# A hybrid attention block on one core: x's first slice in two transfers, small loads moved, first kv products reordered, gate stores on ScalarE's queue, last sum of squares in one step

## The chip, the cores and the metric

The kernel runs on one core of one Trainium2 chip. A core has five engines that run side by side, each with its own instruction queue: TensorE (PE in the profile; PEld is its weight load), VectorE (DVE), ScalarE (ACT), GpSimd (POOL) and SyncE (SP), which here only issues transfers. Transfers may be issued from SP, ACT and POOL; all of them run on the core's 16 DMA engines. The metric is the device time of one execution in microseconds; lower is better.

## The reference

One pre-norm residual layer, 512 tokens, width 1024, all float32. One input projection feeds two token mixers: A, latent attention with 8 heads, dense and causal by chunks of 64; and B, sparse attention, in which an indexer scores the keys, each query keeps its best 128, and a relative-position bias is added. Each branch is gated, projected and weighted by a sigmoid gate; the sum goes through an output projection, the residual is added, and a final RMS norm closes it.

```python
h = rmsnorm(x, norm_g[l])
(q_lat, c_kv, k_rope, z_a, q_b, k_b, v_b, z_b,
 q_idx, k_idx, w_idx, gate_a, gate_b) = jnp.split(h @ w_in[l], cuts, axis=-1)
q = (rmsnorm(q_lat, g_q_lat[l]) @ w_uq[l]).reshape(B, S, MLA_HEADS, MLA_NOPE + MLA_ROPE)
kv = (rmsnorm(c_kv, g_kv_lat[l]) @ w_ukv[l]).reshape(B, S, MLA_HEADS, MLA_NOPE + MLA_V)
...
y_a = mla_attention(q_nope, q_pe, k_nope, k_pe, v_a, pos).reshape(B, S, MLA_WIDTH) * jax.nn.silu(z_a)
y_b = dsa_attention(q_b, k_b, v_b, q_idx, k_idx, w_idx, rel_bias, pos, topk) * jax.nn.silu(z_b)
merged = (jax.nn.sigmoid(gate_a) * (y_a @ w_o_a[l])
          + jax.nn.sigmoid(gate_b) * (y_b @ w_o_b[l]))
x = x + merged @ w_out[l]
return rmsnorm(x, final_g)
```

## The kernel before

Every float32 operand of a product is split into a high part, rounded to TensorE's fast float format (a cast on ACT, L302, or a scaled copy, L311), and a low part, the rest (a subtraction on DVE or POOL, L328 and L330, or DVE's `scalar_tensor_tensor`, L339). A product is then three matmuls (`mm3`): high by high, high by low, low by high. Lines such as L302, L311, L328, L339 and L400 are helpers that record every operation of their kind, so tiles tell more than lines. Large square products (gates, some projections, the output projection) are done in Strassen's way with seven block products instead of eight (`seven`, `output`).

The order of instructions on each engine is fixed when the program is built. Each piece of the work is a generator (a thread) that yields steps with an estimated duration; `Flow.run` simulates the engines with these estimates and always emits the step that can start first, with a small bias for a thread's priority and a tiny random nudge per thread, drawn from a generator seeded with `DRAW`. So any change of a step's estimate, of a thread's steps or of the seed may change the order anywhere. Tiles come from pools of buffers (`slot`, `RAW`, `bank`); a buffer is given back by `put`.

The stages, in order:

- Start. `setup` issues the first index-query weights (`w_qi`, 128 KB) on ACT's queue; `loads` issues on SP, for each of 8 slices k of the model width, x transposed (`xT[k]`, 128 rows of 512 tokens, 256 KB), index weights and kv weights, with `norm_g` behind the first x; `setup_pool` issues the identity matrix (64 KB) and the latent gains (`g_lat`, 2.5 KB) on POOL's queue. `warm_up` runs 15 matmuls on zeros. `early_x` makes scaled high and low parts of each x slice, `early_w` those of the weights.
- `early_mm` multiplies them: index products `qi` (128 by 384 outputs, two groups of three matmuls each slice) and kv products (four token tiles, 328 columns, three matmuls each: 12 a slice), then the q latents. For slice 0 the high part of x is made in three pieces (`PIECES`: tokens 256 to 511, 128 to 255, 0 to 127), so that four high-by-high index matmuls can begin early; the low part is made in one instruction for all 512 tokens, and kv products wait for both parts of x and both parts of the weights.
- In the meantime x is loaded once more by rows, its sums of squares are taken (`x_squares`), and `rstd` is turned and spread over all partitions.
- Middle: normalised x, the remaining projections, the indexer's scores, top-k by repeated maximum on DVE (`topk`), and both kinds of attention heads. The eight tiles of the first sigmoid gate (`w_ga`) are computed early, stored to a scratch area in DRAM (`spilt`) and fetched back when they are needed (`fetch_gates`).
- End: gated branch outputs, output projection, and per token tile t: `finish` adds a block product to the residual (L339), takes a sum of squares into a column of `ssf[t]`, and multiplies by the final gain; `scale_out` adds the partial sums of squares, takes the power -1/2 on POOL (L378), scales both halves (DVE and ACT) and stores them from SP. Tiles 2 and 3 are finished first, then 0 and 1. For tiles 1 and 3 the output's second half arrives in two pieces, so there are three partial sums (`count == 3`), and the third takes an add of its own; the third of tile 1 is the last product of the kernel, and its squares are summed on DVE (`last`), the others on ACT:

```python
        yield ts(rs[:, 0:1], ssf[t][:, 0:1], ssf[t][:, 1:2], D * EPS, ALU.add, ALU.add)
        if count == 3:
            yield is_done(("sq", t, 2))
            yield tt(rs[:, 0:1], rs[:, 0:1], ssf[t][:, 2:3], ALU.add)
        done.add(("sum", t))
        yield power(rs[:, 0:1])
```

`out_job` prepares the blocks of `w_out` and their sums for the output projection.

Of the kernel before, what the change touches and what calls it, by code (L numbers as in the profile page):

```python
# [133 lines left out]
class Flow:  # L134
# [9 lines left out]
    def __init__(self):  # L144
        self.free = {"PE": 0.6, "ACT": 0.6, "DVE": 0.6, "POOL": 0.6, "SP": 0.6}
        self.hw, self.dma = 0.6, 0.0
# [36 lines left out]
    def run(self, stop=None):  # L183
        while self.threads:
# [42 lines left out]
            else:  # L227
# [3 lines left out]
                if step.moves and eng == "ACT":  # L231

                    end += 1.8 + step.moves
# [14 lines left out]
DRAW = 71  # L248
# [4 lines left out]
def tile_block(ctx: ExitStack, tc: tile.TileContext, a: dict, out: bass.AP, bias_dram: bass.AP):  # L253
# [181 lines left out]
    def act_dma(dst, src):  # L435
        step = Step([("ACT", 0.06, lambda: nc.scalar.dma_start(dst.ap, src))], bufs(dst), [])
        step.moves = 4.0 * dst.n * dst.ap.shape[0] / 360000
        return step
# [45 lines left out]
    def setup():  # L484
# [3 lines left out]
        eraw["q", 0] = rq.all.f[:, :256], True  # L488
        yield memset("DVE", zeros.all, 0.0)
# [38 lines left out]
    def loads():  # L528
        for kp in range(4):
            for kk in range(2):  # L530
                k = 2 * kp + kk
                x = yield slot("x")
                yield dma(x.all.f, a["xT"][k])
                xt[k] = x
                if k == 0:
                    yield dma(normg.all, a["norm_g"])
                if kp == 0:
                    cq, ck = slice(256 * kk, 256 * kk + 256), slice(328 * kk, 328 * kk + 328)
                    if k:
                        rq = yield slot("er")  # L540
                        yield dma(rq.all.f[:, :256], a["w_qi"][kp][:, cq])
                        eraw["q", k] = rq.all.f[:, :256], True
# [11 lines left out]
            if kp == XAT:  # L554
                spawn(x_squares(), PSQ)
# [49 lines left out]
    def split_w(raw, w, dst, key, cls="w", cap=None, release=False, early=False):  # L605
# [3 lines left out]
        yield act(hi[:, :w], raw)  # L609
        step = lo_part(lo[:, :w], raw, hi[:, :w])  # L610
# [5 lines left out]
    first_x = {}  # L616

    def early_x():
        for k in range(NK):
            yield Until(lambda: k in xt)  # L620
# [12 lines left out]
    def early_w():  # L633
        for k in range(NK):
# [5 lines left out]
            yield from split_w(raw, 328, ewkv, k, "w", WCAP, last, True)  # L640
# [5 lines left out]
    def early_mm():  # L646
# [6 lines left out]
        for i, piece in enumerate(PIECES[:2]):  # L653
            yield Until(lambda: piece.start in first_x)
# [1405 lines left out]
```

## Time and profile before

| | us |
|---|---|
| median of three timed runs | 427.27 (426.54 to 429.5) |
| the profiled execution, its own time | 427.16 |
| its span, first to last instruction | 425.4 |
| first product on real data | 4.91 |

The profile is one execution. A row of the timeline or of the groups gives start, duration, engine, line, operation, result and operands, shape and count; in brackets the idle time of the engine just before, and what ended it. Matmuls are pipelined and their ends are modelled, so bars of successive matmuls overlap; the distance between starts tells their pace. Rows of a queue (ACTq, SPq) are the issues of transfers, not the moving of data. Reads of the time to landing come from another view: a slice of x takes 4.9 us from issue to landing at the start, a gate store 2.5 us in the middle. The eight gate stores are issued from SP between 55.3 and 196.7 us.

### The profile page before, as it was taken

Reading aid. Unit: us, or ns where it says so; the run is one execution under the profiler, and the core shown is the slowest. Engines: PE = TensorE matmul, PEld = TensorE weight load, DVE = VectorE, ACT = ScalarE, POOL = GpSimd, SP = SyncE. Lnnn points to the kernel's source line nnn. Section 1 sums busy time; section 2 is a strip of 40 time slices with the busy share of each in tenths; the row PEclk is TensorE's granted clock in tenths of the full one; section 3 lists DMA queues with packets and bytes.
Section 4 is the critical chain, followed back from the end, with each engine's and each line's share of the span. In section 5 each row is a group of like instructions: output and inputs, shape, how many; then the busy total and the mean of one; then the engine's idle time right before and its main releaser. Section 6 shows DMA issues by size and latency. Waiting matters only on the chain.

```text
span 425.4 us, 7106 instructions
## 1 busy us (share of the span) xinstructions
PE 415.3 (98%) x2313; PEld 363.9 (86%) x2313; DVE 380.5 (89%) x815; ACT 262.2 (62%) x587; POOL 109.5 (26%) x131
## 2 busy tenths in 40 slices
PE   8999999999999999999999999999999999999993
PEld 6999868889888888888899988998998888888883
DVE  4789899999999999999879888988799757999995
ACT  6778786585573758544864677494598524436624
POOL 1037865455355723121300101000010002210212
PEclk9999999999999999999999999999999999999998
DMA  8973137817255450285243525425523887453705
GB/s 258 394 278 112 52 100 207 230 45 186 82 139 148 127 160 1 79 256 173 63 128 121 171 79 157 146 65 178 146 79 124 266 322 252 143 180 106 242 0 197
DMA packets 30277, 65.89 MB, mean 155 GB/s; under 512 B 4648, under 2 KB 5688, under 8 KB 30240
## 3 DMA queue, kind: packets, MB, share of 16 engines
q1 hardware_dynamic: 29264, 64.08, 48.5%
q0 software_dynamic: 832, 1.22, 0.9%
q8 instruction: 18, 0.29, 0.3%
q14 instruction: 19, 0.16, 0.1%
q10 hardware_dynamic: 144, 0.13, 0.1%
HBM read 50.49 MB, written 4.21 MB: 129 GB/s over the span
## 4 chain that ended last, share of the span: by engine, by line
PE 54%; DVE 30%; DMA 7%; ACT 4%; issue 4%; POOL 0%; POOLq 0%; SPq 0%; DVEq 0%; ACTq 0%
PE ps L400 50%; DVE mask L826 4%; DMA raw<-w_out 4%; DVE sm L825 3%; PE ps L417 2%; DVE sm L1474 2%; DVE s_ph L328 2%; DVE s_mg L328 2%; DVE s_wsum L328 1%; DMA s_sig<-bias_scratch 1%; DVE s_tmp L328 1%; ACT s_p L311 1%; DVE s_pair L328 1%; DVE s_wo L328 1%; DVE s_w L328 1%
## 5 line engine op out<-in xcount | busy, mean ns | idle before, releaser
L400 PE MATMUL ps<-s_h,s_w 128*128 128x512 f32 (+1 forms) x732 | 170.9, 379 | 0.0
L400 PEld LDWEIGHTS ps<-s_h,s_w 128*128 128x128 f32 x732 | 127.8, 189 | 21.8 <-issue 0.3
L302 ACT CAST s_w<-raw 128x512 fp32r<-128x512 f32 (+3 forms) x124 | 71.6, 593 | 17.8 <-DVE raw L328 9.2
L330 POOL TENSOR_TENSOR s_w<-raw,s_w 128x512 fp32r<-128x512 f32 (+2 forms) x35 | 44.7, 1284 | 130.1 <-ACT s_w L302 123.9
L328 DVE TENSOR_TENSOR s_w<-raw,s_w 128x512 fp32r<-128x512 f32 (+2 forms) x89 | 58.7, 670 | 5.3 <-ACT s_w L302 4.7
L400 PE MATMUL ps<-s_ys,s_w 128*128 128x512 f32 x192 | 43.7, 389 | 0.0
L400 PEld LDWEIGHTS ps<-s_ys,s_w 128*128 128x128 f32 x192 | 36.0, 188 | 7.5
L311 ACT ACTIVATE s_p<-s_p,sm 128x384 f32<-128x384 f32 (+3 forms) x54 | 29.2, 559 | 6.8 <-DVE sm L1571 5.6
L400 PE MATMUL ps<-s_wo,s_mg 128*128 128x512 f32 (+1 forms) x156 | 33.0, 373 | 0.0
L400 PE MATMUL ps<-s_w,s_xg 128*128 128x328 f32 (+1 forms) x192 | 32.5, 323 | 0.0
L400 PEld LDWEIGHTS ps<-s_wo,s_mg 128*128 128x128 f32 x156 | 27.6, 188 | 5.2
L400 PEld LDWEIGHTS ps<-s_w,s_xg 128*128 128x128 f32 x192 | 31.4, 188 | 0.0
L328 DVE TENSOR_TENSOR s_ph<-ps,s_ph 128x384 fp32r<-128x384 f32 (+1 forms) x48 | 27.4, 590 | 2.5 <-ACT s_ph L302 2.3
L302 ACT CAST s_ph<-ps 128x384 fp32r<-128x384 f32 (+1 forms) x48 | 23.5, 514 | 5.5 <-PE ps L417 4.2
L311 ACT ACTIVATE s_p<-ps,sm 128x128 f32<-128x128 f32 (+3 forms) x32 | 16.8, 527 | 15.5 <-DVE sm L1474 15.1
L826 DVE MATCH_REPLACE8 mask<-sm,mask 128x384 f32<-128x384 f32 (+2 forms) x48 | 25.8, 540 | 0.0
L825 DVE MAX8 sm<-mask 128x8 f32<-128x384 f32 (+2 forms) x48 | 25.5, 547 | 0.1
L400 PE MATMUL ps<-s_ph,vv 128*128 128x512 f32 (+3 forms) x128 | 24.9, 325 | 0.0
L417 PE MATMUL ps<-ident,s_p 128*128 128x128 f32 x160 | 24.2, 275 | 0.5 <-DVE s_p L358 0.3
L417 PEld LDWEIGHTS ps<-ident,s_p 128*128 128x128 f32 x160 | 18.8, 140 | 4.7 <-ACT s_p L311 1.0
L400 PEld LDWEIGHTS ps<-s_ph,vv 128*128 128x128 f32 x128 | 20.6, 189 | 2.1 <-DVE s_ph L328 0.2
L400 PE MATMUL ps<-s_lat,s_w 128*128 128x512 f32 x78 | 20.5, 398 | 0.0
(197 smaller groups left out, 737.5 us busy)
## 6 DMA issues: line engine op xcount, KB each, us to landing
raw<-w_out SPq DMA_DIRECT2D x18, 512.0 KB, 4.0
s_op<-s_op SPq DMA_DIRECT2D x36, 128.0 KB, 2.3
raw<-w_ga SPq DMA_DIRECT2D x8, 512.0 KB, 4.5
raw<-w_gb SPq DMA_DIRECT2D x8, 512.0 KB, 4.4
raw<-w_o SPq DMA_DIRECT2D x16, 256.0 KB
s_x<-xT SPq DMA_DIRECT2D x8, 256.0 KB, 4.9
s_xn<-x SPq DMA_DIRECT2D x8, 256.0 KB, 5.7
bias_scratch<-s_sig SPq DMA_DIRECT2D x8, 256.0 KB, 2.5
```

The source lines that it names most:

```text
L302: nc.scalar.copy(dst.ap, src.ap)
L311: nc.scalar.activation(dst.ap, src.ap, func, **kw)
L328: opts.append(("DVE", 0.07 + 0.00104 * x.n, lambda: nc.vector.tensor_tensor(dst.ap, x.ap, y.ap, op=op)))
L330: opts.append(("POOL", 0.15 + 0.0021 * x.n, lambda: nc.gpsimd.tensor_tensor(dst.ap, x.ap, y.ap, op=op)))
L400: nc.tensor.matmul(ps.ap, l.ap, r.ap, start=start and i == 0, stop=stop and i == len(pairs) - 1, skip_group_check=more)
L417: nc.tensor.transpose(d.ap, s.ap, ident.tile)
L825: yield Step([("DVE", t, lambda: nc.vector.max(m8.tile, work.tile))], [m8], [work])
L826: yield Step([("DVE", t, lambda: nc.vector.match_replace(work.tile, m8.tile, work.tile, MARK))], [work], [m8])
L1474: yield Step([("DVE", 0.07 + 0.00104 * n, lambda: nc.vector.tensor_reduce(mx.tile[:, 1:2], ps.tile[:, :n], op=ALU.max, axis=AX.X, negate=T ...
```

## The change

- Slice 0 of x is loaded in two transfers: tokens 256 to 511 from SP, tokens 0 to 255 from ACT's queue behind the first index weights; the index weights of slice 1 follow there too. Both halves write the same tile; `x0` holds one dependence record for each.
- The identity and the latent gains are loaded from SP behind the last x slice, no longer from POOL at the start.
- For slice 0 each of the three pieces gets its own low-part instruction (`first_low`), and the third piece waits until the first kv weights have their high part (`first_kv`). The kv products of slice 0 begin with x's high and low parts against the weights' high part, token tiles 3 to 0; x's high part against the weights' low part follows.
- For tile 1, the last piece's sum of squares starts from the sum of the other columns, kept in `partial_sum[t]`, and writes the whole sum; its separate add is gone.
- The eight gate stores, and the store of the second half of tile 1, are issued from ACT's queue.
- In `out_job`, product 4's in-place sum waits until product 6's split of the same buffer is emitted.
- The cost model of transfers issued from ACT is changed, and `DRAW` goes from 71 to 28.

```diff
-DRAW = 71
+DRAW = 28
...
     def act_dma(dst, src):
-        step = Step([("ACT", 0.06, lambda: nc.scalar.dma_start(dst.ap, src))], bufs(dst), [])
+        step = Step([("ACT", 0.41, lambda: nc.scalar.dma_start(dst.ap, src))], bufs(dst), [])
         step.moves = 4.0 * dst.n * dst.ap.shape[0] / 360000
+        return step
+
+    def act_move(dst, src):
+
+        d = dst.ap if isinstance(dst, View) else dst
+        step = Step([("ACT", 0.3, lambda: nc.scalar.dma_start(d, src.ap))], bufs(dst), bufs(src))
+        step.moves = 4.0 * src.n * src.ap.shape[0] / 360000
         return step
...
         eraw["q", 0] = rq.all.f[:, :256], True
+        yield Until(lambda: x0)
+
+        x0.append(Buf(x0[0].tile, "x0"))
+        yield act_dma(x0[1].all.f[:, LO], a["xT"][0][:, LO])
+        xt[0] = x0[0]
+        rq = yield slot("er")
+        yield act_dma(rq.all.f[:, :256], a["w_qi"][0][:, 256:512])
+        eraw["q", 1] = rq.all.f[:, :256], True
...
-        yield Until(lambda: 3 in xt)
-        yield from pool_dma(ident.all, a["ident"])
-        yield from pool_dma(glat.all, a["g_lat"])
...
-                yield dma(x.all.f, a["xT"][k])
-                xt[k] = x
-                if k == 0:
+                if k:
+                    yield dma(x.all.f, a["xT"][k])
+                    xt[k] = x
+                else:
+                    yield dma(x.all.f[:, HI], a["xT"][0][:, HI])
+                    x0.append(x)
                     yield dma(normg.all, a["norm_g"])
...
             if kp == XAT:
+                yield dma(ident.all, a["ident"])
+                yield dma(glat.all, a["g_lat"])
                 spawn(x_squares(), PSQ)
...
-                for piece in PIECES:
-                    yield act(hi[:, piece], xt[k].all.f[:, piece], AF.Copy, scale=normg[:, k : k + 1])
-                    first_x[piece.start] = hi
-                yield stt(lo.all, xt[k].all.f, normg[:, k : k + 1], hi.all.f, ALU.mult, ALU.subtract)
+                for i, piece in enumerate(PIECES):
+                    if i == 1:
+                        yield Until(lambda: 0 in xt)
+                    if i == 2:
+                        yield Until(lambda: first_kv)
+                    x = x0[i > 0].all.f[:, piece]
+                    part = Buf(hi.tile, "xg"), Buf(lo.tile, "xg")
+                    yield act(part[0][:, piece], x, AF.Copy, scale=normg[:, 0:1])
+                    first_x[i] = part
+                    yield stt(part[1][:, piece], x, normg[:, 0:1], part[0][:, piece].f, ALU.mult, ALU.subtract)
+                    first_low.add(i)
...
+                yield Until(lambda: first_kv)
+                wide = slice(0, 328)
+                for t in (3, 2, 1, 0):
+                    i = (2, 1, 0, 0)[t]
+                    yield Until(lambda: i in first_low)
+                    x = cut(first_x[i], TOK[t])
+                    yield mm(kv_ps[t][:, wide], [(x[0], first_kv[0][:, wide]), (x[1], first_kv[0][:, wide])], True, False)
+                yield Until(lambda: k in ewkv)
+                for t in range(NT):
+                    yield mm(kv_ps[t][:, wide], [(first_x[(2, 1, 0, 0)[t]][0][:, TOK[t]], ewkv[k][1][:, wide])], False, False)
...
-                yield dma(spilt(c), s.all.f)
+                yield act_move(spilt(c), s.all.f)
...
-                    yield Until(lambda: 2 * c + i in sums)
+                    yield Until(lambda: 2 * c + i in sums and (product == 6 or (6, 2 * c + i) in right))
...
         if last:
+            yield Until(lambda: t in partial_sum)
+            s = partial_sum[t]
             step = Step([("DVE", 0.1 + 0.00104 * r.n, lambda: nc.vector.tensor_tensor_reduce(
-                junk.tile[:, : r.n], r.ap, r.ap, op0=ALU.mult, op1=ALU.add, scale=1.0, scalar=0.0,
-                accum_out=ssf[t].tile[:, nth : nth + 1]))], [junk, ssf[t]], bufs(r))
+                junk.tile[:, : r.n], r.ap, r.ap, op0=ALU.mult, op1=ALU.add, scale=1.0, scalar=s.tile[:, 0:1],
+                accum_out=s.tile[:, 1:2]))], [junk, s], [r.buf, s])
...
         if count == 3:
-            yield is_done(("sq", t, 2))
-            yield tt(rs[:, 0:1], rs[:, 0:1], ssf[t][:, 2:3], ALU.add)
+            if t < 2:
+
+                partial_sum[t] = rs
+                yield is_done(("sq", t, 2))
+                r = rs[:, 1:2]
+            else:
+                yield is_done(("sq", t, 2))
+                yield tt(r, r, ssf[t][:, 2:3], ALU.add)
         done.add(("sum", t))
-        yield power(rs[:, 0:1])
+        yield power(r)
...
-            yield dma(out[TOK[t], half * 512 : (half + 1) * 512], x)
+            dst = out[TOK[t], half * 512 : (half + 1) * 512]
+            if t == 1 and half:
+
+                yield Step([("ACT", 0.06, lambda: nc.scalar.dma_start(dst, x.ap))], [], bufs(x))
+            else:
+                yield dma(dst, x)
```

More of the change, by code (lines that the diff above doesn't have):

```diff
@@ L231, in run @@
                 if step.moves and eng == "ACT":
[L233 removed]
+                    self.adma = max(self.adma, end + 1.5) + step.moves * (SLOW if end < 7.3 else 1.0)
+                    end = self.adma + 1.0
                 elif step.moves:
@@ L639, in early_w @@
             raw, last = eraw["kv", k]
-            yield from split_w(raw, 328, ewkv, k, "w", WCAP, last, True)
+            yield from split_w(raw, 328, ewkv, k, "w", WCAP, last, True, first_kv)
         for k in range(NK):
@@ L653, in early_mm @@
         for i, piece in enumerate(PIECES[:2]):
-            yield Until(lambda: piece.start in first_x)
+            yield Until(lambda: i in first_x)
             for m in range(2):
-                yield mm(qi_ps[m][:, piece], [(ewq[0][0][:, m * P : m * P + P], first_x[piece.start][:, piece])], not i, False)
+                yield mm(qi_ps[m][:, piece], [(ewq[0][0][:, m * P : m * P + P], first_x[i][0][:, piece])], not i, False)
         for k in range(NK):
+            if k == 0:
+                yield Until(lambda: 1 in first_low)
+                xk = cut(first_x[1], SCORED)
+                w = [cut(ewq[k], slice(m * P, m * P + P)) for m in range(2)]
+                for cw, cx in ((1, 0), (0, 1)):
+                    for m in range(2):
+                        yield mm(qi_ps[m][:, SCORED], [(w[m][cw], xk[cx])], False, False)
+                put(*ewq[k])
+                yield Until(lambda: first_kv)
[8 more added lines that the diff above has]
+                    yield mm(kv_ps[t][:, wide], [(first_x[(2, 1, 0, 0)[t]][0][:, TOK[t]], ewkv[k][1][:, wide])], False, False)
+                put(*ewkv[k])
+                continue
             yield Until(lambda: k in xg and k in ewq)
```

33 lines of the change are left out of this document (15 added, 18 removed).

## The prediction

> **What bounds the kernel now.** I began with the cores' view and the page's busy times.
>
> ```profile
> core 0: 425.4 us, clock 0.995
> ```
>
> ```profile
> PE 415.3 (98%) x2313; PEld 363.9 (86%) x2313; DVE 380.5 (89%) x815; ACT 262.2 (62%) x587; POOL 109.5 (26%) x131
> ```
>
> TensorE is busy for 98% of 425.4 us at practically the full granted clock. The measured time of this execution is 427.16 us, so 1.76 us lie outside the span; the median of the three timed runs is 427.27 us, 0.11 us above it. I make the sum against 427.16 and add 0.11 at the end. Next, the busy time by stretches, cut where the early projections give way to attention, where the long tail of dense products begins, and after the last matmul (columns: stretch, length, then busy us and instruction count of PE, PEld, DVE, ACT, POOL, then clock, DMA share, GB/s):
>
> ```profile
> 46.00:200.00 154.00, 152.77 (x796) 129.25 (x794) 150.59 (x344) 95.81 (x224) 69.54 (x84) 1.00 0.48 137
> 200.00:418.60 218.60, 218.32 (x1257) 192.22 (x1255) 192.71 (x390) 130.53 (x282) 21.29 (x18) 1.00 0.47 147
> 418.60:425.40 6.80, 0.00 (x0) 0.00 (x0) 2.38 (x9) 1.71 (x4) 1.19 (x2) 0.72 0.60 230
> ```
>
> PE loses 1.23 us of 154 in the first stretch and 0.28 us of 218.6 in the second; then come 6.8 us without any matmul. What PE waited for, over the whole span, from the second longest on (the longest is its warm-up's start; columns: who waited, for whom, us in total, times, longest):
>
> ```profile
> PE ps L852 <- DVE mask L339: 1.0, 1, 1.0
> PE ps L400 <- ACT s_xg L311: 0.5, 1, 0.5
> PE ps L417 <- DVE s_p L358: 0.3, 1, 0.3
> PE ps L417 <- ACT s_p L311: 0.2, 1, 0.2
> PE ps L400 <- DVE s_xg L339: 0.2, 1, 0.2
> ```
>
> No DMA is in this list. All of PE's idle time in the middle, 1.0 + 0.3 + 0.2 = 1.5 us, is what better ordering could give there. The diff leaves the number of products as it is: the two index pieces, the four low-part products and the twelve kv products of slice k = 0 are the same instructions in another order. So this kernel is a start, about 412 us of fixed PE work, and a tail, and the change can only shorten the start and the tail, or disturb the middle.
>
> **The start.** PE in order of time, after its warm-up:
>
> ```profile
> 4.91 1.16 PE L400 MATMUL ps<-s_xg,s_w 128*128 128x256 f32 x6 [0.48 <-ACT s_xg L311]
> 6.28 0.62 PE L400 MATMUL ps<-s_xg,s_w 128*128 128x384 f32 x2 [0.21 <-DVE s_xg L339]
> 6.74 1.95 PE L400 MATMUL ps<-s_w,s_xg 128*128 128x328 f32 x12
> 8.52 1.40 PE L400 MATMUL ps<-s_xg,s_w 128*128 128x384 f32 x6
> 9.77 1.96 PE L400 MATMUL ps<-s_w,s_xg 128*128 128x328 f32 x12
> 11.57 1.21 PE L400 MATMUL ps<-s_xg,s_w 128*128 128x384 f32 x6
> 12.61 1.95 PE L400 MATMUL ps<-s_w,s_xg 128*128 128x328 f32 x12
> ```
>
> Dense, the six index products of one slice take 12.61 - 11.57 = 1.04 us and its twelve kv products about 11.57 - 9.77 = 1.80 us. Slice 1's index products took 9.77 - 8.52 = 1.25 us, so 0.21 us was lost there; the wait for the low part of x before 6.28 loses some more. From 11.57 on PE runs without a gap. What ACT does meanwhile:
>
> ```profile
> 0.73 0.41 ACTq L436 DMA_DIRECT2D s_er<-w_qi  x1
> 1.17 1.28 ACT L311 ACT_TABLE_LOAD   x1 [1.17 <-PEq L2052]
> 2.46 0.21 ACT L311 ACTIVATE warm<-neghalf 128x8 f32<-128x8 f32 x1
> 4.04 0.40 ACT L302 CAST s_w<-s_er 128x256 fp32r<-128x256 f32 x1 [1.38 <-DMA s_er<-w_qi]
> 4.36 1.09 ACT L311 ACTIVATE s_xg<-s_x,normg 128x256 fp32r<-128x256 f32 x3
> 5.43 0.47 ACT L302 CAST s_w<-s_er 128x328 fp32r<-128x328 f32 x1
> 7.05 0.72 ACT L311 ACTIVATE s_xg<-s_x,normg 128x512 fp32r<-128x512 f32 x1 [1.15 <-DMA s_x<-xT]
> ```
>
> Two landings rule here: the first index weights at about 4.04, and slice 1 of x at about 7.05, for which ACT sat idle 1.15 us. DMA issues on SyncE up to that slice, the two on GpSimd, and the rate of all transfers in two stretches:
>
> ```profile
> 1.65 0.43 SPq L427 DMA_DIRECT2D s_er<-w_kvl  x1
> 2.12 0.43 SPq L427 DMA_DIRECT2D s_x<-xT  x1
> ```
>
> ```profile
> 1.32 0.76 POOL L431 DMA_DIRECT2D ident<-ident  x1 [0.19 <-issue]
> 2.08 0.56 POOL L431 DMA_DIRECT2D glat<-g_lat  x1
> ```
>
> ```profile
> 2.50:3.50 1.00, 1.00 (x7) 0.73 (x5) 0.00 (x0) 0.17 (x1) 0.14 (x1) 1.00 0.95 324
> 3.50:5.00 1.50, 1.02 (x6) 0.42 (x4) 0.43 (x1) 0.96 (x3) 0.00 (x0) 1.00 0.89 185
> ```
>
> **Part by part.** *First x in two transfers, on two queues.* The first product needs 128 KB of index weights and, now, only the upper 128 KB of x instead of 256 KB (sizes from the shapes in the code): 128 KB less at 324 GB/s is 0.40 us. If the landing is set by fixed delay instead, it is 0. I take 0.3, nearer to the rate, since the engines were 95% busy there; PE then starts near 4.6. ACT's queue gets two more issues of 0.41 us, which push the table load and the dummy exponential to an end at 2.67 + 0.82 = 3.49 us, still ahead of 3.7; that cover is thin, and if the weights landed before 3.49 nothing more would be won.
>
> [...]
>
> In this trace, the far bound is that both halves move at the poor rate of the second stretch: 256 KB take 1.42 us at 185 GB/s against 0.81 us at 324, 0.6 us more, and then the start wins nothing. I put that into a rival.
>
> *Small loads later.* The stretch from 3.5 to 5.0, with the engines 89% busy, moved 185 GB/s and not 324: 1.5 x 139 = 208 KB missing, worth 0.64 us, where the narrow loads (normg, ident, glat) are in flight. Ident's own 64 KB are another 0.20 us. Normg's narrow rows stay, so I credit half of the 0.64. Against that the second index weights (128 KB, 0.40 us) now go ahead of slice 1 on ACT's queue. Net 0.32 + 0.20 - 0.40 = 0.12, and at most 0.44: slice 1 lands 0 to 0.44 us earlier, I take 0.15, near 6.9.
>
> *What is late next.* Slice 0's products can be done near 4.6 + 1.2 + 1.8 = 7.6 now that kv begins with high parts and the low part of x comes in pieces, instead of 8.5. But slice 1 then waits for its x: high part 0.72 us, then DVE's low part. DVE's low part of a whole slice is shown by the chain of waits at the start:
>
> ```profile
> 5.48 0.76 DVE s_xg L339
> ```
>
> So 6.9 + 0.04 + 0.72 + 0.04 + 0.76 = 8.46, and five of the six index products behind it, 5/6 of 1.04 = 0.87, end at 9.33 where kv of slice 1 began at 9.77. The start's gain is 0.44 us, not the 0.9 of slice 0; between 0.3 (x lands as before) and 0.75. I take 0.5, since the second index weights will be split ahead of x on both ACT and DVE. From slice 2 on the stage is PE's, so the gain is carried to the end of that stage. Three low-part instructions instead of one cost DVE some extra fixed time, beside PE work.
>
> *Ident, glat on SyncE behind slice 7.* Two issues of about 0.43 us ahead of the loads for the row sums; those are paced by the bytes, which stay the same. Nothing.
>
> *Gate stores on ACT's queue.* On SyncE they blocked the queue:
>
> ```profile
> SPq L427 <- ACT s_sig L311: 11.9, 4, 7.5
> ```
>
> Up to 7.5 us for the weight loads behind them; but PE waits for no DMA, so freeing it wins nothing. On ACT each costs an issue of 0.41 us (the row at 0.73), eight of them 3.3 us, between 55 and 197 us, where ACT is busy 95.81 of 154 us. Queued behind each store are casts and exponentials that feed PE. With 58 us idle there I take 0; all on the path it is +3.3 us.
>
> *The guard in the weight sums* adds a condition on emission order, no instruction. *The new seed and the changed cost model* re-order the middle. I take 0; bounds are -1.5 (all idle PE time in the middle gone) and +5 (the third rival).
>
> *The tail.* In order of time:
>
> ```profile
> 420.09 0.08 DVE L1768 DVE_READ_ACCUMULATOR2_ANT ssf<- 128x1 f32 x1
> 420.21 0.16 DVE L328 TENSOR_TENSOR sm<-sm,ssf 128x1 f32<-128x1 f32 x1
> 420.29 0.42 DVE L339 SCALAR_TENSOR_TENSOR s_rg<-s_xr,s_fg 128x256 f32<-128x256 f32 x1
> 420.45 0.66 POOL L378 TENSOR_TENSOR sm<-sm,neghalf 128x1 f32<-128x1 f32 x1 [1.32 <-DVE sm L328]
> 421.15 0.72 ACT L311 ACTIVATE s_rg<-s_rg,sm 128x512 f32<-128x512 f32 x1 [1.27 <-POOL sm L378]
> ```
>
> The sum's last add goes: the power starts 0.08 us after its source (420.37 to 420.45), so at 420.25 instead of 420.45: 0.20 us. Of the two last stores, the second was issued late:
>
> ```profile
> 422.09 0.38 SPq L427 DMA_DIRECT2D out<-s_rg  x1
> ```
>
> ```profile
> 422.50:423.90 1.40, 0.00 (x0) 0.00 (x0) 0.00 (x0) 0.00 (x0) 0.00 (x0) 0.50 0.98 372
> ```
>
> ACT could issue it at 421.87, 0.2 us sooner, but both stores (512 KB) already move together at 372 GB/s with the engines 98% busy: the bytes set the end. 0, at most 0.2.
>
> **Sum.** 427.16 - 0.5 - 0.2 = 426.46, plus 0.11: 426.6 us.
>
> **Rivals.** *The early gain is lost* (x in halves moves slowly, or slice 1 lands as before or later): only the tail is left, 427.27 - 0.2 = 427.1. For it: ACT's 1.15 us wait at 7.05 shows which load is late, and 128 KB more go ahead of it. Chance 0.17.
>
> *ACT's stores are on PE's path.* Place: 55 to 197 us. For it: DVE is busy 150.59 of 154 us there and PE's order is fixed, so an exponential late by 0.5 us has no slack on DVE to be caught up; PE did wait 0.2 us for ACT at L417. Against: 58 us of ACT idle, and PE lost just 1.23 us in this stretch. It decides once more than two of the eight stores delay PE (2 x 0.41 exceeds the gain of 0.7): 4 on the path give 426.6 + 1.6 = 428.2, all eight 426.6 + 3.3 = 429.9. Chance 0.14.
>
> [...]
>
> *The new order starves PE behind DVE.* The one long wait of the middle, 1.0 us for DVE's mask at L852, is of this kind; five such waits are 5 us: 431.6. Against: PE has waited so once. Chance 0.08.
>
> *The new order closes PE's gaps*: 426.6 - 1.5 = 425.1, and with the early bound of 0.75 424.8. Chance 0.12. That leaves 0.49 for my forecast, 426.0 to 427.0.
>
> **Numbers.** 426.6; range 424.7 (gaps closed and the better start) to 429.6 (most of the store rival). A measurement of this kernel can tell about 1%, 4.3 us, from no change. Faster than that would need 423.0, below every case but one in which start, gaps and tail all give their bounds: 0.03. Slower than 431.5 takes the DVE rival: 0.08. Within: 0.89.
>
> **What would show it.** Right: first product near 4.6, slice 1's ACT copy no later than 7.05, PE's idle time in 46 to 200 near 1.2 us, no add between accumulator read and power, the last stores still moving at some 370 GB/s. Wrong: a new PE wait on ACT or DVE of a microsecond or more in the middle; or the slice 1 copy after 7.1.

## The result, and the profile after

| us | before | after |
|---|---|---|
| median | 428.02 (426.54 to 430.3, 20 timings) | 430.99 (428.3 to 433.05, 20 timings) |
| ratio to before, 95% interval | | 1.0069 [1.0052, 1.0087] |
| the profiled execution, its own time | 427.16 | 429.51 |
| its span | 425.4 | 427.7 |

The change makes the kernel 0.7% slower. That is within the 1% that the prediction called the likely outcome, but 430.99 lies above its range (424.7 to 429.6), and the sign of its sum (0.7 us faster) is wrong. First the cores' view and the page's busy times of the changed kernel:

```profile
core 0: 427.7 us, clock 0.997
```

```profile
PE 416.0 (97%) x2313; PEld 364.1 (85%) x2313; DVE 379.2 (89%) x805; ACT 264.9 (62%) x596; POOL 111.8 (26%) x131
```

TensorE has the same 2313 matmuls and 0.7 us more of busy time; the rest of the 2.3 us by which the span grew is new idle time. Busy times by stretches (columns as in the prediction, the second cut moved to 420.9, half a microsecond behind this execution's last matmul), and then what PE waited for, without its warm-up:

```profile
46.00:200.00 154.00, 152.62 (x794) 129.11 (x793) 148.64 (x335) 97.03 (x224) 72.53 (x85) 1.00 0.47 133
200.00:420.90 220.90, 219.44 (x1260) 192.74 (x1258) 194.19 (x392) 131.89 (x290) 21.75 (x18) 1.00 0.46 145
420.90:427.70 6.80, 0.00 (x0) 0.00 (x0) 2.44 (x8) 2.06 (x5) 0.67 (x1) 0.82 0.72 271
```

```profile
PE ps L418 <- ACT s_p L312: 0.9, 1, 0.9
PE ps L401 <- ACT s_xg L312: 0.8, 1, 0.8
PE ps L1531 <- issue: 0.7, 1, 0.7
PE ps L1532 <- DMA s_op<-kpel: 0.5, 1, 0.5
PE ps L843 <- DVE mask L340: 0.3, 1, 0.3
PE ps L401 <- ACT s_w L303: 0.2, 1, 0.2
```

The old long wait for DVE's mask has shrunk from 1.0 to 0.3 us, but others have come or grown: at the start (s_xg and s_w, 0.8 and 0.2, where s_xg had 0.5 and 0.2) and three in the middle. PE lost 0.28 us between 200 and 418.6 before; between 200 and 420.9 it now loses 1.46, of which some 0.5 us lie behind its last product. The start, PE in order of time:

```profile
4.64 0.79 PE L401 MATMUL ps<-s_xg,s_w 128*128 128x256 f32 x2 [0.21 <-ACT s_w L303]
6.26 1.19 PE L401 MATMUL ps<-s_xg,s_w 128*128 128x128 f32 x6 [0.82 <-ACT s_xg L312]
7.28 1.95 PE L401 MATMUL ps<-s_w,s_xg 128*128 128x328 f32 x12
9.07 1.20 PE L401 MATMUL ps<-s_xg,s_w 128*128 128x384 f32 x6
10.11 1.95 PE L401 MATMUL ps<-s_w,s_xg 128*128 128x328 f32 x12
```

The first product comes 0.27 us sooner in this execution, near the forecast 4.6, and then PE stops: slice 1's kv products begin at 10.11 instead of 9.77. What held it is in ACT's rows:

```profile
1.17 0.46 ACTq L437 DMA_DIRECT2D s_x<-xT  x1
...
3.79 0.51 ACT L312 ACTIVATE s_xg<-s_x,normg 128x256 fp32r<-128x256 f32 x1 [0.15 <-DMA normg<-norm_g]
4.21 0.39 ACT L303 CAST s_w<-s_er 128x256 fp32r<-128x256 f32 x1
5.44 0.46 ACT L303 CAST s_w<-s_er 128x328 fp32r<-128x328 f32 x1 [0.84 <-DMA s_er<-w_kvl]
5.81 0.40 ACT L312 ACTIVATE s_xg<-s_x,normg 128x128 fp32r<-128x128 f32 x1
```

The second half of x was there, 2.7 us after its issue at 1.17, and its scaling could have followed at 4.6. The plan put the cast of the first kv weights ahead of it in ACT's queue, and that cast waited 0.84 us for its own load; PE's next products waited behind both. The rate of all transfers there:

```profile
2.50:3.50 1.00, 1.00 (x7) 0.73 (x5) 0.00 (x0) 0.99 (x2) 0.00 (x0) 1.00 1.14 307
3.50:5.00 1.50, 1.29 (x6) 0.68 (x5) 0.67 (x2) 0.94 (x3) 0.00 (x0) 1.00 0.90 281
```

Between 3.5 and 5.0 us the transfers now move 281 GB/s where they moved 185, as moving the small loads was meant to bring; no run moves these loads alone. With x in rows of half the length, all transfers together move 307 GB/s between 2.5 and 3.5 us, where they moved 324. The tail in order of time, DVE's last sum into the residual, the squares, the power and the scaling (the fence behind it: the same last sum in the kernel before):

```profile
421.31 0.41 DVE L340 SCALAR_TENSOR_TENSOR s_xr<-ps,s_xr 128x256 f32<-128x256 f32 x1
...
422.44 0.08 DVE L1810 DVE_READ_ACCUMULATOR2_ANT sm<- 128x1 f32 x1
...
422.60 0.67 POOL L379 TENSOR_TENSOR sm<-sm,neghalf 128x1 f32<-128x1 f32 x1 [1.89 <-DVE sm L1810]
423.30 0.72 ACT L312 ACTIVATE s_rg<-s_rg,sm 128x512 f32<-128x512 f32 x1 [1.06 <-POOL sm L379]
```

```profile
419.03 0.41 DVE L339 SCALAR_TENSOR_TENSOR s_xr<-ps,s_xr 128x256 f32<-128x256 f32 x1
```

The add is gone, and from the last sum to the scaling it is 1.99 us (423.30 - 421.31) instead of 2.12 (421.15 - 419.03). But the stores then take 4.40 us to the end of the span instead of 4.25. These two rows, the first kv product of slice 1 and the last residual sum, are recorded starts and not modelled ends, so I use them to cut every profile below into start, middle and tail. For this pair: start +0.34, middle +1.94 (411.20 against 409.26 us), tail +0.02, together the 2.30 us of the spans. The medians differ by 2.97, so the other executions lose 0.6 us more than the profiled ones do.

### The profile page after: what moved, and what is told of

Same layout as the page of the kernel before. It is cut to its first block, busy times and chain, and to the rows that moved or that the text cites. A ratio compares the mean times of both kernels' runs of the same rounds, so it can differ in the third digit from the quotient of the medians.

```text
span 427.7 us, 7106 instructions
## 1 busy us (share of the span) xinstructions
PE 416.0 (97%) x2313; PEld 364.1 (85%) x2313; DVE 379.2 (89%) x805; ACT 264.9 (62%) x596; POOL 111.8 (26%) x131
## 4 chain that ended last, share of the span: by engine, by line
PE 57%; DVE 26%; DMA 6%; issue 4%; ACT 4%; SPq 1%; POOL 1%; POOLq 0%; DVEq 0%; ACTq 0%
PE ps L401 51%; PE ps L418 3%; DVE s_w L329 3%; DVE s_tmp L329 2%; ACT s_p L312 2%; DVE s_mg L329 2%; DVE s_wo L329 2%; DVE s_wsum L329 1%; DVE s_p L329 1%; DMA s_bias<-bias_scratch 1%; DVE sm L1514 1%; DVE s_pair L329 1%; DVE s_ph L329 1%; DVE s_y L329 1%; DMA s_op<-s_op 1%
## 5 line engine op out<-in xcount | busy, mean ns | idle before, releaser
L331 POOL TENSOR_TENSOR s_w<-raw,s_w 128x512 fp32r<-128x512 f32 (+2 forms) x37 | 46.1, 1251 | 122.7 <-ACT s_w L303 97.0
L312 ACT ACTIVATE s_p<-s_p,sm 128x128 f32<-128x128 f32 (+3 forms) x61 | 30.9, 537 | 5.4 <-DVE sm L1611 4.7
L401 PE MATMUL ps<-s_hs,s_w 128*128 128x256 f32 x144 | 21.0, 286 | 0.0
```

What stands on the lines that cost most here:

```text
L312: nc.scalar.activation(dst.ap, src.ap, func, **kw)
L331: opts.append(("POOL", 0.15 + 0.0021 * x.n, lambda: nc.gpsimd.tensor_tensor(dst.ap, x.ap, y.ap, op=op)))
L401: nc.tensor.matmul(ps.ap, l.ap, r.ap, start=start and i == 0, stop=stop and i == len(pairs) - 1, skip_group_check=more)
```

## The experiments

My theory after the two traces had two parts: the order that the planner drew costs the middle its 1.9 us, and the kv cast ahead of the x piece costs the start. The rival causes were the gate stores on ACT, the tail, and the transfers.

**One edit or one draw at a time.** *Gate stores back on SyncE*, everything else in the changed kernel's order:

```diff
-        step = Step([("ACT", 0.3, lambda: nc.scalar.dma_start(d, src.ap))], bufs(dst), bufs(src))
+        step = Step([("ACT", 0.3, lambda: nc.sync.dma_start(d, src.ap))], bufs(dst), bufs(src))
```

> The changed kernel, instruction for instruction in the same order, but its eight gate stores are issued from SyncE at the same places instead of ScalarE. Theory A (the changed order of the middle costs, not the queue of the stores): the ratio to the kernel before stays at 1.005 to 1.009, PE's long waits at about 84, 137 and 205 us stay. Theory B (the stores in ScalarE's queue cost the middle's 1.5 us): ratio 1.0035 or less and the waits for ScalarE at 205 us gone. Rival C (SyncE's queue was better off without them): slower than the changed kernel, over 1.009.

Measured 432.4 (430.22 to 436.38), ratio 1.0103 [1.0059, 1.0147]. Taking the stores off ACT wins nothing. By its number this falls to rival C, but its interval overlaps that of the change, so a loss isn't shown either. The wait for ACT's s_p is 1.6 us here; in four profiles of the changed kernel it is 0.6 to 1.5 us. *The x piece ahead of the kv cast*, by holding back the emission of that cast and its low part:

```diff
+            if step.hold or any(id(x) in late for x in step.ins):
+                self.held.append((step, emit))
+            else:
+                emit()
+            if step.frees:
+                for _, held in self.held:
+                    held()
...
+        step.hold = cast is not None and not cast
...
+                    step.frees = i == 1
```

> The changed kernel in the same order but for the first microseconds: ScalarE's cast of slice 0's kv weights and VectorE's low part of them are put behind the second piece of x. Theory A (ScalarE stood 0.84 us at the head of its queue waiting for kv weights while the second piece of x had landed): the gap of PE between the first two products and the next goes from 1.6 us to under 0.5, kv of slice 1 starts at 9.0 to 9.6 us instead of 10.11, and the total falls by 0.5 to 1.1 us, ratio about 1.005. Rival (the earlier start is taken up by later waits): kv of slice 1 earlier, total unchanged at about 1.007. Rival (slice 1's x sets the time anyway): kv of slice 1 still near 10.

Measured 430.86 (428.38 to 432.44), ratio 1.0046 [1.0025, 1.0068]: the interval overlaps that of the change, so this alone tells nothing, and slice 1's kv products begin at 11.11 and not at 9.0 to 9.6. Its profile held a surprise. PE ran without the gap, and yet slowly:

```profile
4.90 2.50 PE L412 MATMUL ps<-s_xg,s_w 128*128 128x256 f32 x8 [0.46 <-ACT s_w L314]
7.20 3.03 PE L412 MATMUL ps<-s_w,s_xg 128*128 128x328 f32 x12
10.07 1.21 PE L412 MATMUL ps<-s_xg,s_w 128*128 128x384 f32 x6
```

The twelve kv products took 3.03 us where 1.95 is usual. (The end of this execution does not show it: its own time was 429.4.) *The draws exchanged*: the changed kernel with before's number, and the kernel before with the changed kernel's.

```diff
-DRAW = 28
+DRAW = 71
```

> The changed kernel with the old seed 71, so another order of the middle and the end, all edits kept. Theory A (the order that the plan happens to take costs the 2 us of middle and tail): the total moves by a microsecond or more either way against the changed kernel, and its PE waits lie elsewhere. Theory B (the edits themselves cost): the total stays within 0.5 us of the changed kernel, ratio 1.006 to 1.008, with the start's loss the same 0.3 us.

> The kernel before with the seed 28 alone. Theory A (order): it differs from the kernel before by 1 to 3 us, ratio 1.002 to 1.007, with PE waits at other places and perhaps a longer tail. Theory B (the edits): within 0.5 us of the kernel before, ratio 0.999 to 1.001.

The changed kernel with 71: 429.33, ratio 1.0026 [1.0003, 1.0049], an interval just below that of the change. The kernel before with 28, that is with no edit but this number: 435.15, ratio 1.0141 [1.0115, 1.0167]. One number, which adds no instruction, is worth twice the whole result. It changes more than the order: many steps may run on one of several engines, and the planner chooses. With 28 the kernel before has 807 instructions on DVE instead of 815, 136 on POOL instead of 131. Where I write order, I mean the whole plan, the choice of engines with it; the two were not separated. PE's longest waits in the kernel before with 28 show part of the loss:

```profile
PE ps L417 <- ACT s_p L311: 1.7, 2, 1.5
PE ps L803 <- DVE mask L339: 1.3, 1, 1.3
```

**TensorE's pace at the start.** Since slow kv products had appeared, I filled PE's idle gaps with matmuls on zeros, whose results nothing reads. In the kernel before: two more behind the warm-up and two ahead of the low-part products. In the changed kernel: two behind the warm-up and five in the gap. A third kernel holds back the kv cast as above and has two and one; a fourth draws that with 71. The edit of the first, in part:

```diff
+    def fill(ps, n):
+        z = zeros.tile.bitcast(BF16)
+        for _ in range(n):
+            nc.tensor.matmul(ps.tile[:, :256], z[:, :P], z, start=True, stop=True)
...
                 for cw, cx in ((1, 0), (0, 1)):
+                    if cx:
+                        fill(kv_ps[0], 2)
```

> The kernel before in its own order, with four more matmuls on zeros in PE's idle time at the start: two behind the warm-up (to about 4.9 us), two ahead of the products that wait for x's low part. Theory A (TensorE's clock is still at half when an execution's start has too much idle time, by luck of the execution): fewer runs start slow, the median falls by 0.3 to 1.5 us, ratio 0.9965 to 0.9995, first products at full pace (384 columns in 0.175 us). Rival (the clock opens at the same moment whatever PE does): ratio 1.000 to 1.001.

> The changed kernel in its own order, with seven more matmuls on zeros: two behind the warm-up, five in the gap between the first piece's products and the second's. Theory A (the gap of 1.1 us keeps the clock at half in many executions, which is the part of the 3 us that the profiled execution does not show): ratio falls from 1.007 to about 1.003 to 1.005. Rival (the whole loss is in the order of middle and tail and the 0.3 us of the profiled start): ratio stays at 1.006 to 1.008.

> The changed kernel with slice 0's second piece of x ahead of the kv cast on ScalarE and VectorE, and three more matmuls on zeros (two behind the warm-up, one ahead of the first kv product). Theory A: gap gone and clock open, kv of slice 1 starts at 9.0 to 9.5 us as predicted blind (9.3), ratio 1.001 to 1.004, what is left being the order of the middle and the tail (about 2 us). Rival (slice 1's x or its splits are late next): kv of slice 1 near 9.8, ratio 1.004 to 1.006.

> As the run before this one, but with the old seed 71. Theory A (seed 28's order of middle and tail costs about 2 us against seed 71's, and the rest is the start): ratio 0.994 to 1.000, the fastest so far. Rival (the edits cost in the middle under any order): ratio 1.001 or more.

| kernel | median (range) | ratio to before |
|---|---|---|
| before, filled | 427.63 (426.73 to 428.68) | 0.9977 [0.9955, 0.9999] |
| after, filled | 429.97 (429.25 to 432.07) | 1.0031 [1.0012, 1.0051] |
| after, x first, filled | 430.05 (428.54 to 430.5) | 1.0033 [1.0012, 1.0054] |
| the same, drawn with 71 | 429.03 (428.25 to 430.81) | 1.0009 [0.9986, 1.0032] |

Filling brings the changed kernel from 1.0069 to 1.0031; the intervals just fail to meet. Between the two filled kernels 0.5% remains, though slice 1's kv products begin at 10.05 in the one and 10.08 in the other: what remains lies behind the start. Two forecasts missed: with x first, slice 1's kv products begin at 10.02 and not by 9.5, and the fourth kernel, at 1.0009, isn't the fastest. To tie the pace to the time directly, the changed kernel was profiled three times more:

> The changed kernel, unaltered, one more execution with its profile. Timed runs of it lie between 428.3 and 433.05, and the one in its profile (429.51) had TensorE at full pace from about 7.3 us. Theory (the spread is TensorE's pace at the start): where the twelve kv products of slice 0 take 2.9 us or more instead of 1.95, the time is 430.5 or more; where they take about 1.95, 430.0 or less. Rival (the middle takes up whatever the start loses): the time does not go with the pace at the start; a slow start with a time below 430, or a fast one above 431, would show that.

> The changed kernel, unaltered, a second further execution with its profile; theory and rival as for the first: kv products of slice 0 in 2.9 us or more go with 430.5 or more, in about 1.95 us with 430.0 or less, or else the time does not go with the pace at the start.

> The changed kernel, unaltered, a third further execution with its profile; theory and rival as for the first: kv products of slice 0 in 2.9 us or more go with 430.5 or more, in about 1.95 us with 430.0 or less, or else the time does not go with the pace at the start.

The same row, the kv products of slice 0, of the first, second and third further execution:

```profile
8.55 2.78 PE L401 MATMUL ps<-s_w,s_xg 128*128 128x328 f32 x12
```

```profile
7.32 1.95 PE L401 MATMUL ps<-s_w,s_xg 128*128 128x328 f32 x12
```

```profile
8.43 3.48 PE L401 MATMUL ps<-s_w,s_xg 128*128 128x328 f32 x12
```

Their times were 431.87, 429.3 and 435.92. With the profile on record (1.95 us, 429.51) that is four out of four in the order that the theory gives, though four are few; the first, at 2.78 us, fell just short of the 2.9 that I had named. Slice 1's kv products began 2.1 us later in the first than in the profile on record (12.21), and its end came 2.4 us later. In the third they began 3.2 us later (13.30), and the middle lost 3.2 us more. Its waits for ACT's s_p and s_pair, 1.5 and 0.7 us where the profile on record has 0.9 and none, are part of that; the rest I can't name. Not every late start is passed on, either: with x first, unfilled, slice 1's kv products began at 11.11, and the middle, 410.07 us, was 1.1 us shorter. The kernel before can start so too: the profile of the tail experiment, below, whose start is that of before, shows 3.38 us.

**Parts of the change laid on the kernel before.** Its order stays but for the added and dropped rows, save in the last kernel, which is drawn anew. The edit of the second, the gate stores, in part:

```diff
-                yield dma(spilt(c), s.all.f)
+                yield act_gate(spilt(c), s.all.f)
```

> The kernel before in its own order with the tail's two edits alone: the last sum of squares in one step (one VectorE instruction less) and the second half of tile 1 stored from ScalarE's queue. Theory (as predicted blind): the power starts 0.2 us sooner behind the last products, the last bytes set the end, ratio 0.9990 to 1.0000. Rival (the edit itself lengthens the tail, 7.3 us from the last product to the end instead of 6.8): ratio 1.001 or more, tail over 7.1 us in the profile.

> The kernel before in its own order, only the eight gate stores issued from ScalarE at the same places. Theory (ScalarE's queue is no worse a place, as the slower run with the stores put back on SyncE suggests): ratio 0.998 to 1.001. Rival of the prediction (each store holds back work that PE waits for): ratio 1.002 to 1.008, with PE waits for ScalarE between 55 and 197 us.

> The kernel before in its own order with the four extra matmuls on zeros, the tail's edits and the gate stores on ScalarE together: those parts of the change that cost nothing by the theory, without its start and without a new order. Theory: ratio 0.996 to 0.999, faster than both kernels. Rival (each gain is taken up by a later wait): 0.999 or more.

> The kernel before with the four extra matmuls on zeros and a third seed, 5, no other edit. Theory (the order that a seed draws is worth one to some microseconds, and the kernel before has one of the better): ratio 1.001 to 1.012 against 0.9977 with seed 71. Rival (seed 28 was an outlier and orders matter little): ratio 0.997 to 0.9995.

The tail's edit alone: 428.42, ratio 1.0023 [1.0002, 1.0044]; the forecast of at most 1.0000 missed. Both profiles that have the tail's edit without the new start show a PE wait of 0.7 us for ACT's s_pair that the kernel before lacks; the kernel before, filled, has 0.3 without that edit, so I can't say that it is the cause. Gate stores alone: 428.29, ratio 1.001 [0.9989, 1.0032]. Both, filled: 427.77, ratio 0.9987 [0.9971, 1.0003]. The kernel before, filled, with 5 for its draw: 433.18, ratio 1.0128 [1.0102, 1.0154], so 28 is no freak. The stores as ACT issued them, in the second of these kernels:

```profile
L432 ACTq DMA_DIRECT2D bias_scratch<-s_sig x8: 326/328/358, 55.3 to 196.7; - x8
```

**All edits, order of before.** Each step is planned as before, and only what it emits is changed, so that the rows of every engine stand in the old order but for the ones added, removed or cut into pieces; the wait in `out_job`, which concerns the plan alone, is left out. Cut to one of its places:

```diff
+                step = mm3(kv_ps[t][:, :328], cut(xg[k], TOK[t]), cut(ewkv[k], slice(0, 328)), k == 0, k == NK - 1)
+                if k == 0:
+                    (eng, n, _), = step.options
+                    step.options = [(eng, n, lambda t=t: t or high_first())]
+                yield step
```

> All instruction edits of the change (x in two transfers, identity and latent gains behind the fourth slice of x, low parts by pieces, kv products beginning with the high parts, gate stores and the one output store on ACT, last squares in one step) laid by hand into the order of before: TensorE's list of products, and those of DVE and ACT but for the added or shortened rows, are those of before; DRAW stays 71 and nothing is planned anew. The one edit left out is the wait in out_job, which is one of the plan alone. Theory (the order costs, the edits do not): 0.996 to 1.000 of before, 426.3 to 428.2; the x piece now stands ahead of the kv cast, so no gap near 1 us between the first products. Rival (the edits themselves cost, be it the stores on ACT, the tail or the late identity): 1.003 to 1.007, as the changed kernel.

> The kernel above with four more products on zeros on PE, two behind the warm-up and two ahead of the low-part products, as in the filled kernel before (0.9977 of before). Theory (the edits are good for some 0.5 us at the start once the clock is held up): 0.994 to 0.998, 425.6 to 427.2, at or below the filled kernel before. Rival (the edits cost somewhere behind the start): 0.999 or more.

> The changed kernel with the x piece ahead of the kv cast and the gap filled, with DRAW 5: a third order of the same edits beside 28 (1.0033) and 71 (1.0009). Theory (orders differ by up to a per cent or more whatever the edits): outside 1.0000 to 1.0040, on either side, likely above, since 5 gave 1.0128 for the filled kernel before. Rival (orders count for little with these edits): within 1.0000 to 1.0040.

All edits in the old order: 426.32 (425.96 to 429.33), ratio 0.9982 [0.9959, 1.0004]. Its interval lies wholly below that of the change, though the gate stores, the tail's edit and the moved transfers are all in it. Filled: 427.32, ratio 0.999 [0.9972, 1.0009]: filling, which helped both other starts, does not help this one, and the forecast of 0.994 to 0.998 missed. The third draw of the changed kernel, 5: 434.03, ratio 1.0148 [1.012, 1.0177]. PE at the start, and then two rows of ACT, of the kernel with all edits in the old order:

```profile
4.65 1.81 PE L400 MATMUL ps<-s_xg,s_w 128*128 128x256 f32 x8 [0.21 <-ACT s_xg L311]
6.59 1.46 PE L691 MATMUL ps<-s_w,s_xg 128*128 128x328 f32 x8
7.89 0.76 PE L688 MATMUL ps<-s_w,s_xg 128*128 128x328 f32 x4
8.48 1.21 PE L400 MATMUL ps<-s_xg,s_w 128*128 128x384 f32 x6
9.53 1.95 PE L400 MATMUL ps<-s_w,s_xg 128*128 128x328 f32 x12
```

```profile
6.07 0.47 ACT L302 CAST s_w<-s_er 128x328 fp32r<-128x328 f32 x1 [0.89 <-DMA s_er<-w_kvl]
6.77 0.72 ACT L311 ACTIVATE s_xg<-s_x,normg 128x512 fp32r<-128x512 f32 x1 [0.24 <-DMA s_x<-xT]
```

No gap near a microsecond, slice 1 of x taken up at 6.77 instead of 7.05, and slice 1's kv products 0.24 us sooner than before. What its PE waited for in the middle:

```profile
PE ps L897 <- DVE mask L339: 0.9, 1, 0.9
PE ps L417 <- ACT s_p L311: 0.2, 1, 0.2
```

**All orders side by side**, cut at the two rows named above (us; only profiles whose kv products of slice 0 took less than 2.5 us):

| kernel | order | slice 1's kv | last sum | middle |
|---|---|---|---|---|
| before | before's | 9.77 | 419.03 | 409.26 |
| gate stores on ACT | before's | 9.81 | 419.36 | 409.55 |
| before, filled | before's | 10.05 | 419.56 | 409.51 |
| all edits | before's | 9.53 | 418.45 | 408.92 |
| all edits, filled | before's | 9.52 | 418.95 | 409.43 |
| tail and gate stores, filled | before's | 9.59 | 420.06 | 410.47 |
| after | after's | 10.11 | 421.31 | 411.20 |
| after, second more | after's | 10.15 | 421.11 | 410.96 |
| after, filled | after's | 10.08 | 421.82 | 411.74 |
| after, stores on SyncE | after's | 10.24 | 422.01 | 411.77 |
| after, x first, filled | after's | 10.02 | 421.82 | 411.80 |
| after, x first, filled, 71 | a new one | 9.49 | 420.35 | 410.86 |
| before, 28 | a new one | 9.99 | 424.74 | 414.75 |
| before, filled, 5 | a new one | 9.56 | 424.98 | 415.42 |
| after, x first, filled, 5 | a new one | 10.07 | 427.61 | 417.54 |

In before's order the middle takes 408.9 to 410.5 us whichever edits are in it; in the changed kernel's, 411.0 to 411.8; the means of these two groups are 2.0 us apart. In others it takes up to 417.5. The choice of profiles matters: among those left out for their slow start, the kernel before with the tail's edit has 411.06 us, and the changed kernel with x first, unfilled, 410.07, so with these the two groups would overlap.

## Why the prediction was wrong

*What failed first: "The new seed and the changed cost model re-order the middle. I take 0."* It measured +1.94 us in the profiles. That the new plan and not an edit costs it is shown from both sides: all edits in the old order give 0.9982, and the kernel before, planned anew with another number, gives 1.0141 and 1.0128. A plan sets the order and, for many steps, the engine. My bounds for this term, -1.5 to +5, held it, but its likeliest value was taken as nothing, and the range stopped at 429.6, short of the upper bound. The reason is plain now: before's order loses only about 1.5 us of PE in named waits. So a new draw has little to win and much to lose; of the five other orders tried, none had a shorter middle. The profile before showed this in its idle time, which I read only as room for a gain. Where the 1.94 us lie, the two profiles show in part. Between slice 1's kv products and the last matmul PE is idle for 2.32 us instead of 1.48, which is 0.84; its 2273 matmuls there are recorded as busy for 407.95 us instead of 407.32, which is 0.63, and why is open. The last 0.47 lies behind PE: DVE begins its last sum 0.93 us behind the end of the last matmul (420.38) instead of 0.46 (418.57). In the new plan DVE's scaling of another tile (420.79, 0.48 us) stands ahead of it; before, it stood behind (419.36).

*What failed second: "Slice 0's products can be done near 4.6 + 1.2 + 1.8 = 7.6" and the start's "I take 0.5".* The first product came at 4.64, near the forecast, but that was in part luck: in eight profiles that have the new start and no filling it comes between 4.64 and 4.92, half of them later than 4.83, and in four with the old start between 4.80 and 4.91. The products of slice 0 then ran until slice 1's began at 9.07. I had costed the pieces of x as if ACT made one as soon as it landed. ACT's queue had the kv cast ahead of it, which waited for its load until 5.44. Even with x first, in the old order, slice 0 ends near 8.5, because the kv weights landed late there (the cast at 6.07). I had taken that cast's row in the profile before (5.43) as given; in that kernel's profile it came 0.64 us later. The 1.2 us for slice 0's index products was too small as well: all eight took 1.62 us of PE before (6.74 - 4.91, less the wait of 0.21) and 1.81 with all edits in the old order. In one pair of profiles the start's gain is 0.24 us in the old order, just under the lower bound of 0.3 that I had named; in the changed kernel it is -0.34. Executions differ by as much: without slow products in slice 0, slice 1's kv products begin between 9.56 and 10.05 with the old start.

*What the prediction did not have at all: TensorE's pace at the start.* It read PE's pace from one execution. In the changed kernel the gap at the start goes in some executions with a slow TensorE: from 7 us on, the third further profile has five matmuls in each microsecond until 12 us and the first has five or six until 10 us, where the profile on record has eight or nine. The timings agree with that: 14 of its 20 timings lie above 430.5, while before has 4 of 20 above 429. Filling the gap takes 0.4% off. So of the 0.69%, some 0.4% goes with the start, its pace and its gap, and some 0.3 to 0.5% with the plan of what follows; the parts are from different comparisons and need not add up exactly.

*The gate stores* were taken at 0, with 3.3 us as the rival's full price. Eight issues at 0.33 us cost 1.001 [0.9989, 1.0032] in the old order, and putting them back didn't help the new one. So 0 was right within that interval, and the rival's price for all eight, 3.3 us or 0.8%, lies outside it. (A slip in that rival: two stores at 0.41 us already outweigh the gain of 0.7, not only more than two.)

*The tail* was taken at 0.2 us. The power starts 0.08 us behind the accumulator as forecast, but the squares with their new start take 0.48 us instead of 0.42, and 0.13 us remains; the stores behind give it back in the profile on record. The edit alone, at 1.0023 [1.0002, 1.0044], shows no gain. From the last sum to the end of the span, profiles in before's order take 6.34 to 6.37 us without the edit and 6.15 to 6.34 with it, so a gain of 0 to 0.2 us is all that can be said.

*The sum for the edits themselves* was -0.7 us. In the old order they measured 0.9982 of 427.77, -0.8 us, with an interval from -1.8 to +0.2. So the sum was not far off for the edits, and the error was to treat a redrawn plan as the same plan. That the sum agrees so well is partly luck: in that kernel's profile the start gained 0.24 us and not 0.5, and the middle, for which I had 0, gained 0.34. That kernel, at 0.9982, and the kernel before with four more products on zeros, at 0.9977 [0.9955, 0.9999], are the best found; both beat the changed kernel, and only the second beats the one before beyond its interval. Whether `out_job`'s wait matters by itself was not tried.

Of the rivals, the order that starves PE (431.6, a chance of 0.08) came nearest in its number. Its mechanism, five waits of a microsecond for DVE, is not what the waits show: the longest is 0.9 us and for ACT, and the wait for DVE has shrunk.

## What to carry to other kernels

Where a planner draws the order, cost a changed seed or cost model as a term of its own: look at how little the present order loses, and expect a new draw to lose more, as all five did here. To value an edit, lay it into the old order by changing only what a step emits, and draw anew afterwards. And look for what stands ahead in a queue, not only for when the data land: the second half of x had landed, but ACT, in the order that the plan gave it, first waited 0.84 us for the kv weights.

## What the runs showed of the hardware

In these runs TensorE starts below its later pace, and the printed clock doesn't tell it. Before's 15 warm-up products on 256 columns take 3.38 us, 0.225 us each; 22 of that width near the end, on another type, take 2.77, 0.126 each:

```profile
1.05 3.38 PE L498 MATMUL ps<-zeros 128*128 128x256 bf16 x15 [1.05 <-DVE neghalf L454]
...
415.80 2.77 PE L400 MATMUL ps<-s_wo,qhi 128*128 128x256 f32 x22
```

When the pace rises varies between executions of one kernel: twelve kv products took 1.95, 2.78, 1.95 and 3.48 us in four profiles of the changed kernel. The same stretch, PE's row of windows, in the third further profile of the changed kernel (columns: stretch, length, PE busy and count, clock, DMA share, GB/s), and then in the kernel drawn with 71, whose gap at the start was 2.46 us:

```profile
9.00:10.00 1.00, 1.00 (x5) 1.00 1.04 363
```

```profile
9.00:10.00 1.00, 1.00 (x5) 0.50 1.02 336
```

Both ran five matmuls in that microsecond, where before's profile has seven, most of them wider, and the clock reads 1.00 in the one and 0.50 in the other. So at the start the pace is to be read from the distance of the matmuls. The pace varies, from 1.95 to 3.48 us for the same twelve products, and little is at stake: filling gaps at the start is worth 0.2% (before), 0.4% (after) and nothing that shows in the kernel with all edits in the old order. What sets the moment at which the pace rises, no run here shows. For an edit of the start this means that a gap of a microsecond there, as the changed kernel has, goes in some executions with a loss of two microseconds and more behind it: in two of its four profiles slice 1's kv products began 2.1 and 3.2 us later than in the profile on record.
